# The first modulation rows as TensorE products, and the first input in two halves, in a two-block transformer kernel

## The chip, the cores and the metric

The kernel runs on one core of one Trainium2 chip. Its time is the device time of one execution in microseconds (us). Before the change, three runs took 1449.32, 1450.75 and 1452.83 us; the median is 1450.75 us. The profile shown here is of a separate execution.

## What is computed

Two blocks are applied to 256 tokens of width 1024, in float32. The first mixes an mLSTM with a differential attention and ends in a retrieval of experts; the second has a sparse attention, a convolution and a feed-forward part. The change touches only the start of the first block:

```python
def rmsnorm(x, g):
    xf = x.astype(jnp.float32)
    y = xf * lax.rsqrt(jnp.mean(xf * xf, axis=-1, keepdims=True) + EPS)
    return (y * g.astype(jnp.float32)).astype(x.dtype)
...
    mod = jax.nn.silu(c) @ ada_w[l] + ada_b[l]
    sh1, sc1, g1, sh2, sc2, g2 = jnp.split(mod[:, None, :], 6, axis=-1)

    h = rmsnorm(x, norm1_g[l]) * (1.0 + sc1) + sh1
    p = h @ w_in[l]
    mq, mk, mv, mo, mi, mf, dq, dk, dv = jnp.split(p, split_pts, axis=-1)
```

`ada_w` is 1024 x 6144. `sh1` and `sc1`, the first 2048 of its columns, are needed before the first input `h`; seen as columns of 128 these are 16 "modulation rows", rows 0 to 7 for the shift and 8 to 15 for the scale. The other rows are needed later.

## The kernel before

Everything is held with the features on the 128 partitions: `x` is 8 chunks of 128 x 256. A product in full precision is made of three (`mm3`, L156 to L161): both operands are split into a high and a low part (`hi`, `lo` for the input, `whi`, `wlo` for the weights), and high x high, low x high and high x low are added in PSUM. Weights come by DMA in pairs of units of 128 x 1024 into three buffers named `raw` (`load`, L92). ScalarE (ACT) makes `whi` (L108), VectorE (DVE) makes `wlo` (L116), or both for a few units (L106). `fill` (L97) loads ahead and splits ahead; `w` calls it whenever a unit is taken. Each engine runs its instructions in the order in which they are written, and all loads of this stage are issued from SyncE's queue (SP), in one order.

The start of the first block (`block1_mix`, L419) goes as follows. `silu(c)` is formed on all partitions from a broadcast load of `c` (L430, `silu_vec`). For each modulation row DVE multiplies a 128 x 1024 tile of the transposed `ada_w` with it and sums along the row (`mod_chunk`, L322). The eight scale rows come first, from the `raw` buffers. ACT and TensorE (PE) form the mean square of `x` (`mean_sq`, L280), ACT and DVE its reciprocal root (L257 to L266). Then four times, for two chunks each (L484 to L500): DVE forms two shift rows, ACT forms `hi` (L496), DVE forms `lo` (L499) and scales the next chunks (L481).

`token_major` (L401) multiplies the input with the four units of `w_mv` into two PSUM banks (the tiles named `a`), eight steps k, and behind each step come three products for the gates (`gate`, L512, with `wgate`). Then follow `gates` (L515 to L534), and eight units of `w_mqk`, whose results go through a short convolution (`conv`, tile `cacc`, L550 to L558). The two PSUM banks for units (tiles `m`) come free when `conv` has read them. The rows 16 to 39 are formed later, as chores between units (`mod_chores`, L325).

Of the kernel before, what the change touches and what calls it, by code (L numbers as in the profile page):

```python
# [13 lines left out]
F32 = mybir.dt.float32  # L14
# [5 lines left out]
AF = mybir.ActivationFunctionType  # L20
OP = mybir.AluOpType
# [4 lines left out]
T = 256  # L26
D = 1024
# [28 lines left out]
for _n, _w in (("norm1_g", 8), ("norm2_g", 8), ("final_g", 8), ("norm_mix_g", 8), ("norm_ffn_g", 8),  # L56
               ("ada_b", 48), ("b_ada", 48), ("conv_w", 32), ("conv_b", 8),
               ("mlstm_norm_g", 4), ("diff_norm_g", 1), ("gate_b", 2), ("w_dw", 124), ("b_dw", 4),
               ("conv_ln_g", 4), ("conv_ln_b", 4)):
    SMALL[_n] = (_o, _o + _w)  # L60
    _o += _w
NSMALL = _o
# [2 lines left out]
class Kx:  # L65
# [235 lines left out]
    def pair(self):  # L301
        return [self.normp.tile([128, 8, T], F32R, name=n) for n in ("hi", "lo")]
# [116 lines left out]
    def block1_mix(self):  # L419
        nc, tc, a = self.nc, self.tc, self.a  # L420
        self.mod = [self.const.tile([128, 48], F32, name=f"mod{i}") for i in range(2)]
        mt = self.mod[0]
        with ExitStack() as ctx:
            big = ctx.enter_context(tc.tile_pool(name="b1", bufs=1))
            tmp = ctx.enter_context(tc.tile_pool(name="b1t", bufs=2))
            h = hi, lo = self.pair()
            self.setup()
            self.setup_rows(big)
            craw = tmp.tile([128, D], F32, name="mraw", bufs=2)
            nc.sync.dma_start(craw, self.c_rows(0))  # L430
            self.silu_c[0] = tmp.tile([128, D], F32, name="silu", bufs=1)
            self.silu_vec(0, craw)
            ada = a["ada_w"]
            pair = lambda u: ada[u:u + 2].rearrange("u p f -> p u f")
            held = [big.tile([128, 8, T + 2], F32, name=f"hold{j}") for j in range(4)]
            hold = [t.rearrange("p k t -> p (k t)")[:, :2048].rearrange("p (u f) -> p u f", u=2) for t in held]
            wg = big.tile([128, 8, 36], F32, name="wgate")
            lq = big.tile([128, 4, 64], F32, name="lq")

            def sc_load(j):  # L440
                t = self.wraw.tile([128, 2, 1024], F32, name="raw")
                nc.sync.dma_start(t, pair(8 + 2 * j))
                return t

            sc = [sc_load(j) for j in range(2)]
            nc.sync.dma_start(self.x, a["x"])
            sc.append(sc_load(2))
            nc.sync.dma_start(self.small, a["small"])
            nc.sync.dma_start(wg, a["w_gate"])
            for j in range(4):  # L450
                if j == 3:
                    self.lnexp()
                for i in (1, 0):
                    self.mod_chunk(0, 8 + 2 * j + i, sc[j][:, i], tmp)
                if j == 0:
                    sc.append(sc_load(3))
                elif j == 1:
                    self.load("w_mv", 0)
                    for d in (0, 1):
                        nc.sync.dma_start(hold[d], pair(2 * d))  # L460
                elif j == 2:
                    self.load("w_mv", 2)
                    for d in (2, 3):
                        nc.sync.dma_start(hold[d], pair(2 * d))
                    nc.sync.dma_start(lq, bass.AP(tensor=a["lam"].tensor, offset=a["lam"].offset,
                                                  ap=[[0, 128], [64, 4], [1, 64]]))
            ps = self.side()[:, :T]
            for c in range(8):
                self.mean_sq(ps, self.x[:, c], c, 8, tmp)
            rs = self.rsqrt_start(ps, [128, T], self.normp)  # L470
            rstd = self.rsqrt_end(rs)
            self.mod_bias(0, 8, 16)
            gn = self.make_gain(0, mt[:, 8:16], self.sm("norm1_g"))
            xs = big.tile([128, 8, T], F32, name="xs", tag="yhi")
            wgh = big.tile([128, 8, 36], F32R, name="wgate_h")
            wgl = big.tile([128, 8, 36], F32R, name="wgate_l")
            self.split(wgh, wgl, wg)

            def scaled(j):
                for c in range(2 * j, min(2 * j + 2, 8)):  # L480
                    nc.vector.scalar_tensor_tensor(xs[:, c], self.x[:, c], gn[:, c:c + 1], rstd,  # L481
                                                   op0=OP.mult, op1=OP.mult)

            for j in range(4):  # L484
                if j == 0:
                    self.fill(2, 2)
                elif j == 2:
                    self.fill(4, 4)
                cs = (2 * j, 2 * j + 1)
                if j == 0:  # L490
                    scaled(0)
                for c in reversed(cs):
                    self.mod_chunk(0, c, hold[j][:, c % 2], tmp)
                self.mod_bias(0, cs[0], cs[1] + 1)
                for c in cs:
                    nc.scalar.activation(hi[:, c], xs[:, c], AF.Identity, bias=mt[:, c:c + 1])  # L496
                scaled(j + 1)
                for c in cs:
                    nc.vector.scalar_tensor_tensor(lo[:, c], xs[:, c], mt[:, c:c + 1], hi[:, c].bitcast(F32),  # L499
                                                   op0=OP.add, op1=OP.subtract)  # L500
            heads = lambda t: t.rearrange("p (c t) -> p c t", t=T)

            vm, vd = (hold[0][:, i].rearrange("p (s c) -> p s c", s=2) for i in range(2))
# [2 lines left out]
            ig, fx, ab, B, aa, M, em = (R(n) for n in ("ig", "fx", "ab", "B", "aa", "M", "em"))  # L506
            lf, m = fx, ab
            acol = big.tile([128, 2, 4], F32, name="acol")

            gr = self.side()  # L510

            def gate(k):  # L512
                self.mm3(gr[:36, :T], (wgh[:, k], wgl[:, k]), (hi[:, k], lo[:, k]), k == 0, k == 7)

            def gates():  # L515
                nc.vector.tensor_scalar(ig, gr[:4, :T], gb[:4, 0:1], None, op0=OP.add)
# [16 lines left out]
                yield  # L533
                nc.vector.tensor_copy(acol, p[:, :8].rearrange("p (s h) -> p s h", s=2))  # L534

            self.token_major("w_mv", h, vm, iter([0] * 4), gate)
            self.chores.extend(self.mod_chores([(0, u) for u in range(16, 40)], tmp, 2, nc.sync))
            self.tasks.append(gates())
            self.tick(0)

            qk = [heads(hold[1][:, i]) for i in range(2)]
            cw, cb = self.sm("conv_w"), self.sm("conv_b")
# [86 lines left out]
            for u in range(8):  # L629
                p = self.unit("w_mqk", u, h)  # L630
# [5 lines left out]
            lam = big.tile([128, 2], F32, name="lam")  # L636
# [8 lines left out]
            dg = big.tile([128, 1], F32, name="dg")  # L645
# [72 lines left out]
            for u in range(8):  # L718
                p = self.unit("w_dqk", u, h)
# [3 lines left out]
                else:  # L723
                    for i in range(2):
                        r = slice(64 * i, 64 * i + 64)
# [4 lines left out]
            for u in range(4):  # L730
                p = self.unit("w_mo", u, h)
# [19 lines left out]
            gn = self.make_gain(1, mt[:, 32:40], self.sm("norm2_g"))  # L751
# [752 lines left out]
def _vec(v):  # L1504
    return v.reshape(-1, 128).T


def prepare(**i):
    i = {k: np.asarray(v) for k, v in i.items()}
    w = i["w_in"][0]  # L1510
    o = {}
# [10 lines left out]
    def half(a):  # L1522
# [2 lines left out]
    o["x"] = i["x"][0].T.reshape(8, 128, T).transpose(1, 0, 2)  # L1525
    o["c"], o["c_2"] = i["c"], i["c_2"]
    o["ada_w"] = i["ada_w"][0].T.reshape(48, 128, D)
    o["w_ada"] = i["w_ada_2"][0].T.reshape(48, 128, D)
    g = np.zeros((D, 36), np.float32)
    g[:, :4], g[:, 32:] = mi, mf  # L1530
# [9 lines left out]
    w = i["w_in_2"][0]  # L1540
    q, k, v, qi, ki, wi, ua, ug, ga, gb = np.split(
        w, [512, 1024, 1536, 2048, 2112, 2120, 2632, 3144, 4168], axis=1)
# [5 lines left out]
    f = i["w_ffn_in_2"][0]  # L1548
# [3 lines left out]
    s = np.zeros((128, NSMALL), np.float32)  # L1552

    def put(name, v):
        a, b = SMALL[name]
        s[:v.shape[0], a:b] = v
# [12 lines left out]
    a, b = SMALL["gate_b"]  # L1569
# [2 lines left out]
    put("b_dw", _vec(i["b_dw_2"][0]))  # L1572
    put("conv_ln_g", _vec(i["conv_ln_g_2"][0]))
    put("conv_ln_b", _vec(i["conv_ln_b_2"][0]))
    o["small"] = s
    o["gf"] = i["norm_final_g_2"].reshape(1, D)
    return {k: np.ascontiguousarray(v) for k, v in o.items()}
# [21 lines left out]
```

## Time and profile before

| | before |
|---|---|
| median of three runs | 1450.75 us |
| the profiled execution | 1445.74 us |
| its span, first to last instruction | 1443.7 us |
| PE busy | 1367.2 us, 95% of the span |
| DVE busy | 1098.1 us, 76% |
| ACT busy | 770.9 us, 53% |
| POOL busy | 115.4 us, 8% |
| SP's DMA queue, share of 16 engines | 49.5% |

The span lies 2.0 us below the execution's own time, and that execution lies 5.0 us below the median. Times below are us from the span's start. In a row of the timeline the first number is the start, the second the length, "x2" the number of instructions merged in it, and the bracket the idle time of the engine before it and what ended it. A PE row's length includes the end of the pipeline; from one start to the next is what a product costs in a stream. A float32 product leaves two records on PE, one in the split format leaves one.

### The profile page before, as it was taken

The page shows a single profiled execution, that of the slowest core. Times are in us where ns is not written, and L with a number is a line of the kernel's source. Part 1 is how long each engine was busy: PE and PEld are TensorE (multiplying, and loading weights), DVE is VectorE, ACT ScalarE, POOL GpSimd, SP SyncE. Part 2 cuts the span into 40 slices and gives each one's busy share as a digit, 9 for nine tenths or more (in the row PEclk, how much of TensorE's full clock was granted, in tenths as well). Part 3 has the DMA queues.
Part 4 walks back from the last instruction along what each step waited for, and adds up shares of the span by engine and source line. Part 5 has one row for each costly group of instructions (what it writes and reads, how often), then busy time and mean ns, then how long its engine had stood idle before and what let it go on. Part 6 is the DMA issues. An engine that isn't in the chain of part 4 may idle for free.

```text
span 1443.7 us, 27450 instructions
## 1 busy us (share of the span) xinstructions
PE 1367.2 (95%) x11208; PEld 1321.7 (92%) x11208; DVE 1098.1 (76%) x2105; ACT 770.9 (53%) x1247; POOL 115.4 (8%) x93
## 2 busy tenths in 40 slices
PE   3888999989999999999999999999999899999997
PEld 2767889979999999999999999999999889999997
DVE  7887899996999487777777766666799968765554
ACT  3535665444999545454444454444565484644442
POOL 0020010000000000000000000000167620100000
PEclk8999999999999999999999999999999999999999
DMA  9566554544777888888888867766445335345551
GB/s 376 182 210 216 207 178 147 177 145 146 263 275 280 321 307 291 297 305 315 306 295 283 287 228 240 235 218 219 144 163 175 117 109 208 123 175 190 180 196 64
DMA packets 106062, 317.31 MB, mean 220 GB/s; under 512 B 5584, under 2 KB 34640, under 8 KB 103632
## 3 DMA queue, kind: packets, MB, share of 16 engines
q1 hardware_dynamic: 65696, 250.54, 49.5%
q10 hardware_dynamic: 39408, 61.87, 12.2%
q0 software_dynamic: 832, 3.15, 0.7%
q8 instruction: 88, 1.44, 0.4%
q14 instruction: 38, 0.31, 0.1%
HBM read 297.71 MB, written 17.83 MB: 219 GB/s over the span
## 4 chain that ended last, share of the span: by engine, by line
PE 71%; DVE 21%; ACT 3%; DMA 3%; issue 2%; POOL 0%; POOLq 0%; DVEq 0%; SPq 0%; ACTq 0%
PE m L159 12%; PE m L160 12%; PE m L161 12%; PE a L160 11%; PE a L161 10%; PE a L159 10%; DVE wlo L116 5%; DVE a L1168 3%; DVE junk L322 2%; PE s L983 2%; DMA raw<-in_ada_w 1%; DMA mraw<-in_ada_w 1%; DVE score L1127 1%; DVE cacc L552 1%; ACT whi L108 1%
## 5 line engine op out<-in xcount | busy, mean ns | idle before, releaser
L159 PE MATMUL m<-hi,whi 128*128 128x256 f32 x1816 | 519.3, 286 | 7.1 <-DVE cacc L552 4.0
L161 PE MATMUL m<-hi,wlo 128*128 128x256 f32 x1816 | 509.8, 281 | 2.8 <-POOL wlo L116 1.5
L160 PE MATMUL m<-lo,whi 128*128 128x256 f32 x1816 | 509.6, 281 | 0.0
L116 DVE TENSOR_TENSOR wlo<-raw,whi 128x1024 fp32r<-128x1024 f32 x398 | 479.0, 1222 | 36.3 <-ACT whi L108 25.8
L108 ACT CAST whi<-raw 128x1024 fp32r<-128x1024 f32 x428 | 444.4, 1045 | 50.9 <-DMA raw<-in_peer_v 17.9
L159 PEld LDWEIGHTS m<-hi,whi 128*128 128x128 f32 x1816 | 343.7, 189 | 10.0 <-issue 4.2
L161 PEld LDWEIGHTS m<-hi,wlo 128*128 128x128 f32 x1816 | 343.3, 189 | 3.4 <-DVE wlo L116 1.7
L160 PEld LDWEIGHTS m<-lo,whi 128*128 128x128 f32 x1816 | 343.3, 189 | 0.6
L161 PE MATMUL a<-wh,wlo 128*128 128x256 f32 x1024 | 288.3, 282 | 0.0
L160 PE MATMUL a<-wl,whi 128*128 128x256 f32 x1024 | 288.2, 281 | 0.0
L159 PE MATMUL a<-wh,whi 128*128 128x256 f32 x1024 | 287.9, 281 | 0.0
L161 PEld LDWEIGHTS a<-wh,wlo 128*128 128x128 f32 x1024 | 192.9, 188 | 0.0
L160 PEld LDWEIGHTS a<-wl,whi 128*128 128x128 f32 x1024 | 192.7, 188 | 0.0
L159 PEld LDWEIGHTS a<-wh,whi 128*128 128x128 f32 x1024 | 192.6, 188 | 0.0
L1024 DVE TENSOR_TENSOR wl<-act,wh 128x256 fp32r<-128x256 f32 x128 | 54.5, 425 | 140.5 <-PE a L160 125.2
L790 ACT ACTIVATE act<-m 128x256 f32<-128x256 f32 x126 | 48.4, 384 | 167.2 <-PE m L161 167.2
L1019 ACT CAST wh<-act 128x256 fp32r<-128x256 f32 x128 | 51.9, 406 | 145.4 <-DVE act L1012 121.5
L322 DVE SCALAR_TENSOR_TENSOR junk<-mraw,silu 128x1024 bf16<-128x1024 f32 x80 | 97.5, 1219 | 7.5 <-DMA mraw<-in_ada_w 6.9
L116 POOL TENSOR_TENSOR wlo<-raw,whi 128x1024 fp32r<-128x1024 f32 x33 | 79.2, 2425 | 36.0 <-ACT whi L108 26.5
L986 ACT ACTIVATE stg<-s 128x512 f32<-128x512 f32 x64 | 64.2, 1108 | 3.1 <-PE s L983 1.0
L1012 DVE TENSOR_TENSOR act<-act,gt 128x256 f32<-128x256 f32 x128 | 53.6, 419 | 8.2 <-DMA gt<-gd 8.2
L159 PE MATMUL a<-fh,whi 128*128 128x256 f32 x176 | 50.6, 287 | 3.4 <-ACT fh L250 3.4
(443 smaller groups left out, 1772.8 us busy)
## 6 DMA issues: line engine op xcount, KB each, us to landing
raw<-in_peer_u SPq DMA_DIRECT2D x64, 1024.0 KB, 6.0
raw<-in_peer_v SPq DMA_DIRECT2D x64, 1024.0 KB, 5.1
mraw<-in_w_ada ACTq DMA_DIRECT2D x48, 512.0 KB, 5.5
raw<-in_w_ffn_in SPq DMA_DIRECT2D x22, 1024.0 KB, 5.1
gd<-stg ACTq DMA_DIRECT2D x16, 1024.0 KB, 6.2
gt<-gd ACTq DMA_DIRECT2D x14, 1024.0 KB, 7.5
mraw<-in_ada_w SPq DMA_DIRECT2D x24, 512.0 KB, 4.4
raw<-in_w_ffn_out SPq DMA_DIRECT2D x11, 1024.0 KB, 4.9
```

The costliest lines, as they stand in the source:

```text
L108: self.nc.scalar.copy(t, self.raw[k])
L116: eng.tensor_tensor(t, self.raw.pop(k), h.bitcast(F32), op=OP.subtract)
L159: mm(out, w[0], x[0], start=start, stop=False, **kw)
L160: mm(out, w[0], x[1], start=False, stop=False, **kw)
L161: mm(out, w[1], x[0], start=False, stop=stop, **kw)
L322: self.nc.vector.scalar_tensor_tensor(junk, w, 0.5, self.silu_c[i], op0=OP.mult, op1=OP.mult, accum_out=self.mod[i][:, u:u + 1])
L790: nc.scalar.activation(t, p, AF.Gelu)
L986: nc.scalar.mul(stg[:, :, e0:e0 + 4].rearrange("p i t -> p t i"), p, 1.0 / GSCALE)
L1012: nc.vector.tensor_tensor(tv, tv, gv, op=OP.mult)
L1019: nc.scalar.copy(wts[b], acts[b])
L1024: nc.vector.tensor_tensor(wl, acts.pop(b), wts[b].bitcast(F32), op=OP.subtract)
L1168: nc.vector.scalar_tensor_tensor(zp, z[:, c, k:k + T], w, zp, op0=OP.mult, op1=OP.add)
```

## The change

The 16 rows are formed on PE: the matrix, in its own order, is the moving operand (`ada_n`, cut into eight tiles of 128 x 4 x 512), and `silu(c)`, held as one column of a 32-wide stationary tile (`pad`, tile `junk`) whose other columns are zero, is the stationary one. Four products write to the four quarters of 32 partitions of one PSUM bank, each over half of the sum; ACT copies the bank (L484), and four products with a column of 0.5 turn it into four modulation rows (L487). `row_group(kind, i)` does that for scale (kind 0) or shift (kind 1) of half i. The input is formed in two halves of four chunks (`inputs`), each followed by its half of the products with `w_mv`. `silu(c)` on all partitions, still needed for the later rows, is made between the halves from eight scaled identity blocks and two products with `mean_d` (L530 to L539). `c` is read as a part of `small`.

```diff
+            nc.sync.dma_start(self.small, a["small"])
             nc.sync.dma_start(self.x, a["x"])
+            src = [[rows[:2], rows[2:]]]
+            for kind in range(2):
+                for hf in range(2):
+                    nc.sync.dma_start(src[0][kind][hf], a["ada_n"][(4, 0)[kind] + hf])
+            self.load("w_mv", 0)
             nc.sync.dma_start(wg, a["w_gate"])
-                for i in (1, 0):
-                    self.mod_chunk(0, 8 + 2 * j + i, sc[j][:, i], tmp)
...
+            def row_group(kind, i):
+                g = self.bank(2 + kind)
+                for hf in range(2):
+                    for j in range(4):
+                        mm(g[32 * j:32 * j + 32], pad[:, 4 * hf + j], src[i][kind][hf][:, j], start=hf == 0,
+                           stop=hf == 1, skip_group_check=True)
+                s = tmp.tile([128, 1024], F32, name="mraw", bufs=2)[:, :512]
+                nc.scalar.copy(s, g)
+                p = self.side()
+                for j in range(4):
+                    mm(p[:, j:j + 1], s[:, j * 128:(j + 1) * 128], half, start=True, stop=True, skip_group_check=True)
...
+            def inputs(i):
+                cs = range(4 * i, 4 * i + 4)
                 for c in cs:
-                    nc.scalar.activation(hi[:, c], xs[:, c], AF.Identity, bias=mt[:, c:c + 1])
-                scaled(j + 1)
-                for c in cs:
-                    nc.vector.scalar_tensor_tensor(lo[:, c], xs[:, c], mt[:, c:c + 1], hi[:, c].bitcast(F32),
-                                                   op0=OP.add, op1=OP.subtract)
+                    nc.vector.tensor_scalar(xs[:, c], xs[:, c], gn[:, c:c + 1], mt[:, c:c + 1],
+                                            op0=OP.mult, op1=OP.add)
+                    nc.scalar.copy(hi[:, c], xs[:, c])
+                    if c % 2:
+                        for d in (c - 1, c):
+                            nc.vector.tensor_tensor(lo[:, d], xs[:, d], hi[:, d].bitcast(F32), op=OP.subtract)
...
+            for i in range(2):
+                row_group(0, i)
+                row_group(1, i)
+                if i == 0:
+                    rows_late()
+                    self.split(wgh, wgl, wg)
+                    self.load("w_mv", 2)
+                inputs(i)
+                self.fill(2 * i + 2, 2 * i + 2)
+                for u in (2 * i, 2 * i + 1):
+                    w = self.ready["w_mv", u]
+                    for k in (2 * u, 2 * u + 1):
+                        m = slice(k % 2 * 512, k % 2 * 512 + 512)
+                        for tt in range(2):
+                            s = slice(tt * 128, (tt + 1) * 128)
+                            self.mm3(acc[tt], (hi[:, k, s], lo[:, k, s]), (w[0][:, m], w[1][:, m]), k == 0, k == 7)
+                        gate(k)
+                if i == 0:
+                    dg = tmp.tile([128, 1024], F32, name="mraw", bufs=2)
+                    for k in range(8):
+                        nc.vector.tensor_scalar(dg[:, k * 128:(k + 1) * 128], self.ident, pad[:, k, 0:1], None,
+                                                op0=OP.mult)
+                    self.silu_c[0] = tmp.tile([128, D], F32, name="silu", bufs=1)
+                    for q in range(2):
+                        m = slice(q * 512, q * 512 + 512)
+                        p = self.bank(2 + q)
+                        mm(p, self.mean_d, dg[:, m], start=True, stop=True, skip_group_check=True)
+                        nc.scalar.mul(self.silu_c[0][:, m], p, float(D))
+            for u in range(4):
+                self.w("w_mv", u, False)
...
-            self.token_major("w_mv", h, vm, iter([0] * 4), gate)
-            self.chores.extend(self.mod_chores([(0, u) for u in range(16, 40)], tmp, 2, nc.sync))
+            for tt in range(2):
+                nc.scalar.copy(vm[:, tt], acc[tt])
             self.tasks.append(gates())
             self.tick(0)
+            self.fill(self.pos + 3, self.pos + 2)
+            self.chores.extend(self.mod_chores([(0, u) for u in range(16, 40)], tmp, 2, nc.sync))
```

On SP, the first loads before (`c`, scale rows in `raw`, `x`) stood in this order:

```order
L430 DMA mraw<-in_c 128x1024
L442 DMA raw<-in_ada_w 128x2x1024 x2
L446 DMA x<-in_x 128x2048
L442 DMA raw<-in_ada_w 128x2x1024
L448 DMA small<-in_small 128x319
L449 DMA wgate<-in_w_gate 128x288
L442 DMA raw<-in_ada_w 128x2x1024
L92 DMA raw<-in_w_mv 128x2x1024
```

Now, on SP from its first load on (the four `hold` tiles take the first half's rows):

```order
L441 DMA small<-in_small 128x327
L442 DMA x<-in_x 128x2048
L446 DMA hold_127<-in_ada_n 128x2048
L446 DMA hold_128<-in_ada_n 128x2048
L446 DMA hold_129<-in_ada_n 128x2048
L446 DMA hold_130<-in_ada_n 128x2048
L92 DMA raw<-in_w_mv 128x2x1024
L448 DMA wgate<-in_w_gate 128x288
L454 DMA raw<-in_ada_n 128x2048 x2
```

`x` moved to second place, the scale and shift rows of the first half stand before the first weights, and those of the second half behind.

On PE, the products of the kernel before, from the last mean square on, follow each other with nothing else between them (here the first step of `w_mv` and the start of the second):

```order
L280 MATMUL s<-sq,mean_d 128x256 x8
L159 MATMUL a_283<-whi,hi 128x512
L160 MATMUL a_283<-wlo,hi 128x512
L161 MATMUL a_283<-whi,lo 128x512
L159 MATMUL a_284<-whi,hi 128x512
L160 MATMUL a_284<-wlo,hi 128x512
L161 MATMUL a_284<-whi,lo 128x512
L159 MATMUL s<-hi,wgate_h 36x256
L160 MATMUL s<-lo,wgate_h 36x256
L161 MATMUL s<-hi,wgate_l 36x256
L159 MATMUL a_283<-whi,hi 128x512
```

Now, on PE between the fourth step and the fifth (the bank `a_313` collects scale rows, `a_331` shift rows):

```order
L161 MATMUL m<-hi,wgate_l 36x256
L538 MATMUL a_307<-mraw,mean_d 128x512
L538 MATMUL a_310<-mraw,mean_d 128x512
L481 MATMUL a_313<-raw,junk 32x512 x8
L487 MATMUL s<-half,mraw 128x1 x4
L481 MATMUL a_331<-hold_127,junk 32x512 x4
L481 MATMUL a_331<-hold_128,junk 32x512 x4
L487 MATMUL s<-half,mraw 128x1 x4
L159 MATMUL a_188<-whi,hi 128x512
```

The products that make the second half's modulation rows stand behind the whole first half of the products with `w_mv`, and before the whole second half.

On ACT, around the end of the products with `w_mv`, there stood before (`hold_132` takes the two banks):

```order
L496 ACTIVATE hi<-xs,mod_83 128x256 x4
L108 CAST whi<-raw 128x1024 x2
L496 ACTIVATE hi<-xs,mod_83 128x256 x4
L108 CAST whi<-raw 128x1024 x3
L416 COPY hold_132<-a_283 128x512
L416 COPY hold_132<-a_284 128x512
L517 ACTIVATE fx<-s,small 4x256
```

Now, on ACT over the same place (`hold_127` takes the two banks):

```order
L484 COPY mraw<-a_313 128x512
L484 COPY mraw<-a_331 128x512
L499 CAST hi<-xs 128x256 x4
L108 CAST whi<-raw 128x1024 x2
L575 COPY hold_127<-a_188 128x512
L575 COPY hold_127<-a_189 128x512
L555 ACTIVATE fx<-m,small 4x256
L556 ACTIVATE ab<-fx 4x256
L557 ACTIVATE ab<-ab 4x256
L558 ACTIVATE ab<-ab,one 4x256
L108 CAST whi<-raw 128x1024 x4
```

The splits of the first `w_mqk` units moved from before the copies of the two banks to behind the gates' four ACT instructions, and those of the last two `w_mv` units to behind the last four `hi`.

## Rows read from the trace of the kernel before

**Rows 1.** The chain that ended last, first 130 us: start, length, what.
```profile
8.19 1.24 DVE junk L322 x2
...
41.92 1.15 DVE junk L322 x2
```

**Rows 2.** The timeline of PE, 12 to 50 us.
```profile
29.85 0.80 PE L159 MATMUL a<-whi,hi 128*128 128x512 f32 x1 [10.26 <-ACT hi L496]
...
33.21 0.63 PE L159 MATMUL a<-whi,hi 128*128 128x512 f32 x1
...
35.27 0.39 PE L159 MATMUL a<-whi,hi 128*128 128x512 f32 x1
...
37.01 0.39 PE L159 MATMUL a<-whi,hi 128*128 128x512 f32 x1
...
48.65 0.28 PE L161 MATMUL s<-hi,wgate_l 128*36 128x256 f32 x1
```

**Rows 3.** Busy time by stretch: PE, PEld, DVE, ACT, POOL, granted clock, DMA share, GB/s.
```profile
20.00:30.00 10.00, 0.15 (x1) 0.15 (x1) 9.79 (x22) 3.55 (x7) 0.00 (x0) 0.68 1.03 415
```

**Rows 4.** DMA issues up to 70 us: tile, queue, count, KB each, median us to landing.
```profile
raw<-in_ada_w SPq DMA_DIRECT2D x4, 1024.0 KB, 8.6
...
x<-in_x SPq DMA_DIRECT2D x1, 1024.0 KB, 10.9
...
mraw<-in_c SPq DMA_DIRECT2D x1, 512.0 KB, 4.4
```

**Rows 5.** The timeline of ACT, 12 to 56 us.
```profile
13.16 0.72 ACT L279 ACTIVATE sq<-x 128x256 f32<-128x256 f32 x2 [5.53 <-DMA x<-in_x]
...
19.63 0.47 ACT L257 ACTIVATE rs_t<-s,eps 128x256 f32<-128x256 f32 x1 [0.79 <-PE s L280]
...
21.66 1.99 ACT L108 CAST whi<-raw 128x1024 fp32r<-128x1024 f32 x2 [0.78 <-DMA raw<-in_w_mv]
...
48.21 1.05 ACT L416 COPY hold<-a 128x512 f32<-128x512 f32 x2
50.95 0.47 ACT L517 ACTIVATE fx<-s,small 4x256 f32<-4x256 f32 x1 [1.69 <-DVE ig L516]
...
52.77 1.04 ACT L108 CAST whi<-raw 128x1024 fp32r<-128x1024 f32 x1
```

**Rows 6.** PE, 1175 us: two interleaved column halves (L1302) between other products.
```profile
1175.34 0.28 PE L161 MATMUL m<-hi,wlo 128*128 128x256 f32 x1
1175.55 0.67 PE L1302 MATMUL s<-aTt,v 128*64 128x128 f32 x8
1176.14 0.44 PE L1295 MATMUL s<-ident,S 128*128 128x128 f32 x2
```

**Rows 7.** PE, 1159 us: four float32 products over all 128 columns.
```profile
1159.02 2.00 PE L1187 MATMUL s<-lsq,mean_c 128*128 128x256 f32 x8
```

**Rows 8.** The timeline of DVE, 20 to 57 us.
```profile
22.85 0.16 DVE L349 TENSOR_TENSOR mod<-mod,small 128x8 f32<-128x8 f32 x1
...
23.13 0.45 DVE L251 TENSOR_TENSOR wgate_l<-wgate,wgate_h 128x288 fp32r<-128x288 f32 x1
23.50 2.35 DVE L116 TENSOR_TENSOR wlo<-raw,whi 128x1024 fp32r<-128x1024 f32 x2
...
52.89 0.41 DVE L522 SCALAR_TENSOR_TENSOR fx<-fx,ab 4x256 f32<-4x256 f32 x1 [0.84 <-ACT ab L520]
...
55.87 1.50 DVE L552 SCALAR_TENSOR_TENSOR cacc<-m,small,cacc 128x255 f32<-128x255 f32 x3
```

**Rows 9.** DVE's groups by shape: an operation with two scalars on 128 x 256.
```profile
L1148 DVE TENSOR_SCALAR score<-score 128x256 f32<-128x256 f32 x1 | 0.3, 279 | 0.0
```

**Rows 10.** PE by stretch: length, busy (count), granted clock, DMA share, GB/s.
```profile
20.00:23.60 3.60, 0.00 (x0) 1.00 1.03 420
23.60:30.00 6.40, 0.15 (x1) 0.50 1.03 413
...
33.90:40.00 6.10, 5.02 (x26) 1.00 0.93 343
```

More of the change, by code (lines that the diff above doesn't have):

```diff
@@ L58 @@
                ("mlstm_norm_g", 4), ("diff_norm_g", 1), ("gate_b", 2), ("w_dw", 124), ("b_dw", 4),
-               ("conv_ln_g", 4), ("conv_ln_b", 4)):
+               ("conv_ln_g", 4), ("conv_ln_b", 4), ("c_col", 8)):
     SMALL[_n] = (_o, _o + _w)
@@ L428, in block1_mix @@
             self.setup_rows(big)
[L429 to L434, printed above, removed]
+            flat = lambda t: t.rearrange("p k t -> p (k t)")[:, :2048]
+            quad = lambda t: t.rearrange("p (k f) -> p k f", k=4)
@@ L435, in block1_mix, with row_raw @@
             held = [big.tile([128, 8, T + 2], F32, name=f"hold{j}") for j in range(4)]
-            hold = [t.rearrange("p k t -> p (k t)")[:, :2048].rearrange("p (u f) -> p u f", u=2) for t in held]
+            hold = [flat(t).rearrange("p (u f) -> p u f", u=2) for t in held]
+            rows = [quad(flat(t)) for t in held]
             wg = big.tile([128, 8, 36], F32, name="wgate")
             lq = big.tile([128, 4, 64], F32, name="lq")
-            def sc_load(j):
+            def row_raw():
@@ L441, in sc_load @@
                 t = self.wraw.tile([128, 2, 1024], F32, name="raw")
-                nc.sync.dma_start(t, pair(8 + 2 * j))
-                return t
-            sc = [sc_load(j) for j in range(2)]
+                return quad(t.rearrange("p u f -> p (u f)"))
+            nc.sync.dma_start(self.small, a["small"])
             nc.sync.dma_start(self.x, a["x"])
-            sc.append(sc_load(2))
-            nc.sync.dma_start(self.small, a["small"])
-            nc.sync.dma_start(wg, a["w_gate"])
@@ L450, in block1_mix @@
-            for j in range(4):
-                if j == 3:
-                    self.lnexp()
-                for i in (1, 0):
-                    self.mod_chunk(0, 8 + 2 * j + i, sc[j][:, i], tmp)
[L455 to L466, printed above, removed]
+            src = [[rows[:2], rows[2:]]]
@@ new lines, in block1_mix, with rows_late @@
+            for kind in range(2):
+                for hf in range(2):
+                    nc.sync.dma_start(src[0][kind][hf], a["ada_n"][(4, 0)[kind] + hf])
+            self.load("w_mv", 0)
+            nc.sync.dma_start(wg, a["w_gate"])
+            src.append([[row_raw(), row_raw()], rows[:2]])
+            def rows_late():
+                for kind in range(2):
+                    for hf in range(2):
+                        nc.sync.dma_start(src[1][kind][hf], a["ada_n"][(6, 2)[kind] + hf])
@@ L467, in block1_mix @@
+            pad = tmp.tile([128, 16, 32], F32, name="junk", bufs=1)[:, :8]
+            nc.vector.memset(pad, 0.0)
+            cc = self.sm("c_col")
+            half = big.tile([128, 1], F32, name="half")
+            nc.vector.memset(half, 0.5)
+            ct = tmp.tile([128, 8], F32, name="mx", bufs=4)
+            nc.scalar.activation(ct, cc, AF.Tanh, scale=0.5)
+            nc.vector.scalar_tensor_tensor(pad[:, :, 0], ct, 1.0, cc, op0=OP.add, op1=OP.mult)
+            self.lnexp()
             ps = self.side()[:, :T]
@@ L471, in block1_mix @@
             rstd = self.rsqrt_end(rs)
-            self.mod_bias(0, 8, 16)
-            gn = self.make_gain(0, mt[:, 8:16], self.sm("norm1_g"))
             xs = big.tile([128, 8, T], F32, name="xs", tag="yhi")
@@ L476, in block1_mix @@
             wgl = big.tile([128, 8, 36], F32R, name="wgate_l")
[L477 to L494, printed above, removed]
-                for c in cs:
-                    nc.scalar.activation(hi[:, c], xs[:, c], AF.Identity, bias=mt[:, c:c + 1])
-                scaled(j + 1)
-                for c in cs:
-                    nc.vector.scalar_tensor_tensor(lo[:, c], xs[:, c], mt[:, c:c + 1], hi[:, c].bitcast(F32),
-                                                   op0=OP.add, op1=OP.subtract)
+            mm = nc.tensor.matmul
@@ new lines, in block1_mix @@
+            bias, g1 = self.sm("ada_b"), self.sm("norm1_g")
+            gn = self.gain[:, :8]
+            def row_group(kind, i):
+                g = self.bank(2 + kind)
+                for hf in range(2):
+                    for j in range(4):
[6 more added lines that the diff above has]
+                    mm(p[:, j:j + 1], s[:, j * 128:(j + 1) * 128], half, start=True, stop=True, skip_group_check=True)
+                r = slice((8, 0)[kind] + 4 * i, (8, 0)[kind] + 4 * i + 4)
+                nc.vector.tensor_tensor(mt[:, r], p[:, :4], bias[:, r], op=OP.add)
+                if kind == 0:
+                    nc.vector.scalar_tensor_tensor(gn[:, 4 * i:4 * i + 4], mt[:, r], 1.0, g1[:, 4 * i:4 * i + 4],
+                                                   op0=OP.add, op1=OP.mult)
@@ new lines, in block1_mix, with gate @@
+            gr = self.main()
+            acc = [self.bank(0), self.bank(1)]
+            def gate(k):
+                self.mm3(gr[:36, :T], (wgh[:, k], wgl[:, k]), (hi[:, k], lo[:, k]), k == 0, k == 7)
+            for c in range(8):
+                nc.vector.tensor_tensor(xs[:, c], self.x[:, c], rstd, op=OP.mult)
+            for i in range(2):
[26 more added lines that the diff above has]
+                        nc.scalar.mul(self.silu_c[0][:, m], p, float(D))
@@ L501, in block1_mix @@
+            for u in range(4):
+                self.w("w_mv", u, False)
+            nc.sync.dma_start(lq, bass.AP(tensor=a["lam"].tensor, offset=a["lam"].offset,
+                                          ap=[[0, 128], [64, 4], [1, 64]]))
             heads = lambda t: t.rearrange("p (c t) -> p c t", t=T)
@@ L508, in block1_mix @@
             acol = big.tile([128, 2, 4], F32, name="acol")
-            gr = self.side()
-            def gate(k):
-                self.mm3(gr[:36, :T], (wgh[:, k], wgl[:, k]), (hi[:, k], lo[:, k]), k == 0, k == 7)
             def gates():
@@ L1527, in prepare @@
     o["ada_w"] = i["ada_w"][0].T.reshape(48, 128, D)
+    o["ada_n"] = i["ada_w"][0][:, :2048].reshape(2, 4, 128, 4, 512).transpose(3, 0, 2, 1, 4).reshape(8, 128, 4, 512)
     o["w_ada"] = i["w_ada_2"][0].T.reshape(48, 128, D)
@@ L1574, in prepare @@
     put("conv_ln_b", _vec(i["conv_ln_b_2"][0]))
+    put("c_col", _vec(i["c"][0]))
     o["small"] = s
```

## The prediction

> **What bounds the kernel now.** I read the chain of waits first, then the timelines of the engines on it, in the first 60 us; the part behind them is looked at only for the price of column-packed products. The chain [rows 1] runs from 8.19 to past 41.92 us through the sums on DVE that make the modulation rows; in 20 to 30 us DVE is busy for 9.79 of 10 us and PE for 0.15 [rows 3]. PE starts on `w_mv` at 29.85 us, having waited 10.26 us for the input, and ends the last gate product at 48.65 + 0.28 = 48.93 us [rows 2]; call that point E. From E on, the chain goes through the gates, first on ACT and then on DVE, until DVE starts the first convolution (`cacc`) at 55.87 us [rows 8], 6.94 us behind E. The table in front puts PE at 95% of the whole span, with every stage fed by the one ahead. So a shift of that first `cacc` is a shift of the end unless something later absorbs it, and I work out where E and `cacc` come to lie.
>
> **The change: what goes.** Sixteen sums on DVE (1.15 to 1.24 us each [rows 1]), about 19 us, and the broadcast load of `c`. DVE is then no longer what the input waits for. What is late next is a chain that goes from PE to ACT to PE to DVE to ACT, once for each half.
>
> **Up to the first half's input.** `x` was in at 13.16 us [rows 5], behind 0.52 + 2 x 1.05 MB; with itself 3.67 MB [rows 4]. Now only `small` (0.17 MB) stands ahead: 1.22 MB. At 415 GB/s [rows 3] the 2.45 MB less are 5.9 us: 7.3 us. The next 1.05 MB tiles come 2.5 us apart: the scale rows by 12.4, the shift rows by 17.4, `w_mv` by 19.9, `wgate` by 20.3 us.
> The mean squares are unchanged: 19.63 - 13.16 = 6.47 us from `x` to the end on PE [rows 5], so 13.8 us. A float32 product of 256 columns leaves two records, and eight records take 2.00 us with the pipeline's end [rows 7], about 0.21 us each, or 0.43 for 512 columns. Do four products to four column quarters run side by side? The nearest row has two halves: eight records of 128 columns in 0.67 us [rows 6]. Less the end of the last (0.28), that is four steps of 0.11 us, so they ran in pairs; eight in a row would take 0.75 to the last start alone. I take four side by side: two sets of two records of 0.43, so 1.7 us for a `row_group`, and with switch and end 1.9. The bounds are 3.6 (two by two) and 7.0 (one by one), and nothing better than 1.7, since each set streams 512 columns twice.
> ACT's copy of a 128x512 bank is 1.05 / 2 [rows 5], 0.6 with the handover. The four products with a column of 0.5 leave eight records, each with 128 columns of weights; nearest is the 0.11 us step of rows 6, with the end 1.1 us; bounds 0.5 and 2.
> All of it is serial, because PE runs in program order and the four small products stand ahead of the shift rows: 13.8 + 1.9 + 0.6 + 1.1 = 17.4 for the scale, + 3.6 = 21.0 for the shift. Adding the bias takes 0.16, the split of `wgate`, which stands ahead of the input on DVE, 0.45 [rows 8]: 21.6 us. The input: scaling at 0.28 [rows 9] twice, `hi` at about 0.45 on ACT (taken as `fx` [rows 5]), `lo` as much; the fourth `hi` ends 2.8 us later, 24.4. Only then does ACT split the first weights, 1.99 / 2 us [rows 5], and DVE takes 2.35 / 2 for `wlo` [rows 8]: PE starts at 25.4, and goes on in earnest at 26.6. That is 4.5 us earlier than 29.85.
>
> **The first half, and what stands behind it.** A step k costs 37.01 - 35.27 = 1.74 us at the full clock [rows 2]; four, less the one product done ahead, 6.8: 33.4 us. Two float32 products of 512 columns for `silu`: 1.7, 35.1. Their DVE part (eight 128x128 scalings, under 0.28 each [rows 9]) lies beside the first half. Then the second half's row groups: 2 x (1.9 + 0.6 + 1.1) = 7.2, 42.3. Their data are there (by 30.5 us at the rate above), but PE reaches them only now, and nothing covers them: bias 0.2, input 2.8, `whi` 1.0, `wlo` 1.2, 47.5. The second half 6.8: E at 54.3, against 48.93: **5.4 us later**. The second `w_mv` load on SP waits for the first pair's `wlo` (about 28 us), and all that is queued behind it with it; it lands by 33 us, well ahead of 46.3, so that wait costs nothing. The first two chore loads now stand on SP behind the first `w_dv` load, whose buffer comes free with a `w_mqk` `wlo`, 8 us behind E; the chore that uses them is written behind the fifth convolution, so I count nothing, and a late one would add to the rivals below.
>
> **Behind E.** Before, ACT had split the first `w_mqk` units ahead of E. Now these splits stand behind the two copies and the gates' four ACT instructions. Those wait for the gate products: E + 0.75 for `ig` on DVE, then 1.8 us (52.77 - 50.95 [rows 5]), then 1.0 for the first `whi`: E + 3.6. DVE has four `wlo` in its queue ahead of the gates' second part: 4 x 1.18 = 4.7, E + 8.3. From there to `cacc` it is 55.87 - 52.89 = 3.0 [rows 8]: E + 11.3 in place of 6.94, **4.4 us later**. PE's first two units end by then, so they are hidden.
>
> **The clock.** Before, PE's last mean square ended at 19.6, and the granted clock was still 1.00 up to 23.6 and 0.50 (1.2 GHz) from there; at 33.9, 4 us into the products, it was 1.00 (2.4 GHz) again [rows 10]. Now PE idles from 21.0 to 25.4 and from 42.3 to 46.3. The first gap is longer than those 4.0 us, so I count a fall there: a step then costs 33.21 - 29.85 = 3.36 us [rows 2], and four us at that level, of which 1.2 are waiting, lose 1.5. The second gap is just as long as 4.0; I count nothing, and hold 1.5 as a bound.
>
> **The sum:** 5.4 + 4.4 + 1.5 = 11.3 us later. On the profiled execution that is 1445.74 + 11.3 = 1457.0; that execution lies 5.0 below the median of the runs, so for the median 1450.75 + 11.3 = **1462 us**.
>
> Two rules of the Trainium skill bear on the packed products. The page "TensorE: Matmul & The Clock Gate" (Part 3, Packing small matmuls) states 2.38x for three column tiles. Worked from that figure as an estimate, a group is 1.7 x 3 / 2.38 = 2.2 us and the sum 2 us larger; the pairs of rows 6 show no such loss. Against this change speaks "TensorEngine Tiling (Array Packing)" (Tiling Modes, Key Properties): a change of tiling mode drains TensorE. The trace agrees in kind: from the product at 1175.34 to the first packed one 0.21 us pass [rows 6] in place of 0.12, so eight switches cost under 1 us.
>
> **Rivals.**
> *The products don't run four wide.* Two by two adds 1.7 us to each of four groups: 11.3 + 6.8 = 18.1, 1469 us; one by one adds 5.1 each, 1482. For it: no row here has four quarters, nor 512 float32 columns in each. Against it: the pairs of rows 6.
> *DVE decides after all: faster.* If E is set by DVE's work alone, as rows 1 and 3 show for before, DVE loses 19 us and gains about 2.2 for eight scalings of the input and 1.6 for the identity blocks. E is then some 15 us earlier, less 4.4 behind it: 1440 us. It decides from the point where E falls under 48.9 - 4.4 = 44.5 us. Against it: the second half's `whi` alone can't end before 46.3 in the chain above, and only if PE took the second groups ahead of the first half would that chain shorten; it runs in order.
> *A later stage absorbs it.* The convolutions after 55.87 and the chores wait for loads; where a load isn't later than before, its wait takes up the shift. That gives 1450 to 1457 us. Against it: those loads need buffers that the same chain frees.
>
> **Chances and range.** Forecast 0.64, not four wide 0.15, absorbed 0.11, DVE 0.10. The low end of the forecast's own range has `x` 1 us earlier, small products of 0.5 us (4 x 0.6), and no fall of the clock: +6.4; the high end a second fall: +12.8, and small products of 2 us: +16.4. The range reaches up to two by two and down a little into the absorbed case: 1455 to 1469. About 0.2% (2.9 us) is what a measurement of this kernel can tell from no change. Slower by more: 0.64 + 0.15 + 0.06 of the absorbed case = 0.85; within: 0.05; faster: 0.10.
>
> **What would show it.** PE's first `w_mv` product at 25 to 26 us, an idle stretch of some 4 us on PE between the second half's small products and the fifth step, E at 54 to 56, and ACT's first `w_mqk` split 3 to 4 us behind E, with `cacc` near 67 us. A `row_group` of about 1.9 us shows the packing; 3.6 or 7 the first rival. E under 45 us would make the forecast wrong in its sign, and a later `cacc` with an unchanged end would show absorption.

## The result, and the profile after

| | before | after |
|---|---|---|
| median, 6 runs each on the same chip | 1450.92 us | 1463.16 us |
| lowest to highest | 1449.32 to 1456.25 | 1459.82 to 1466.63 |
| ratio | | 1.0087 (95%: 1.0069 to 1.0105) |
| the profiled execution | 1445.74 | 1462.69 |
| mean granted clock in it | 0.985 | 0.974 |
| first `cacc` on DVE | 55.87 | 69.87 |

The kernel is 12.2 us slower by the medians, where 11.3 were forecast. The profiled execution of after lies 0.5 us below its median, that of before 5.2 below its own. So the two profiles are 17.0 us apart at the end, and the sum is better read at the first `cacc`.

The chain that ended last now begins like this (start, length, what; its pieces of 1.24 us and more, up to 70 us):

```profile
1.26 5.09 DMA x<-in_x
6.84 4.28 PE s L280 x10
13.04 1.90 PE a L481 x16
16.66 1.90 PE a L481 x16
24.47 1.24 DVE wlo L116
35.17 1.72 PE a L538 x4
36.89 1.90 PE a L481 x16
40.55 1.90 PE a L481 x16
48.11 1.24 DVE wlo L116
62.35 4.63 DVE wlo L116 x4
```

None of the sums of [rows 1] is left in it. Instead it goes twice through two row groups (`a` L481) and a `wlo`, and behind the second half through four `wlo` in a row. The timeline of PE at these places (start, length, engine, line; in brackets the idle time before and what ended it):

```profile
12.97 1.92 PE L481 MATMUL a<-hold,junk 128*32 128x512 f32 x16
15.61 1.05 PE L487 MATMUL s<-half,mraw 128*128 128x1 f32 x8 [0.71 <-ACT mraw L484]
...
24.49 0.80 PE L159 MATMUL a<-whi,hi 128*128 128x512 f32 x1 [4.22 <-ACT whi L108]
...
35.01 1.88 PE L538 MATMUL a<-mraw,mean_d 128*128 128x512 f32 x4
36.82 1.92 PE L481 MATMUL a<-raw,junk 128*32 128x512 f32 x16
...
43.11 1.05 PE L487 MATMUL s<-half,mraw 128*128 128x1 f32 x8 [0.70 <-ACT mraw L484]
48.13 0.80 PE L159 MATMUL a<-whi,hi 128*128 128x512 f32 x1 [3.96 <-ACT whi L108]
...
58.42 0.28 PE L159 MATMUL m<-hi,wgate_h 128*36 128x256 f32 x1
```

PE starts 5.4 us earlier than in [rows 2], waits 4 us twice, and its last gate product ends at about 58.94 us (three of them follow at 0.12): E is 10.0 us later. Behind E, on ACT and then on DVE:

```profile
57.93 1.28 ACT L575 COPY hold<-a 128x512 f32<-128x512 f32 x2 [8.90 <-PE a L161]
59.48 0.47 ACT L555 ACTIVATE fx<-m,small 4x256 f32<-4x256 f32 x1 [0.28 <-DVE ig L554]
...
61.29 3.87 ACT L108 CAST whi<-raw 128x1024 fp32r<-128x1024 f32 x4
```

```profile
62.35 4.63 DVE L116 TENSOR_TENSOR wlo<-raw,whi 128x1024 fp32r<-128x1024 f32 x4 [2.30 <-ACT whi L108]
66.90 0.41 DVE L560 SCALAR_TENSOR_TENSOR fx<-fx,ab 4x256 f32<-4x256 f32 x1
...
69.87 1.50 DVE L592 SCALAR_TENSOR_TENSOR cacc<-m,small,cacc 128x255 f32<-128x255 f32 x3
```

From E to `cacc` it is now 10.93 us in place of 6.94 [rows 8]: 4.0 us more. The clock, by stretch (PE busy, granted clock, DMA share, GB/s):

```profile
20.30:24.50 4.20, 0.01 (x1) 0.56 1.02 425
24.50:31.00 6.50, 6.04 (x15) 0.50 0.99 376
31.00:35.00 4.00, 4.00 (x23) 0.99 0.22 70
...
44.20:48.10 3.90, 0.00 (x0) 0.57 0.13 51
48.10:55.20 7.10, 6.61 (x18) 0.52 0.43 148
55.20:59.00 3.80, 3.74 (x21) 1.00 0.00 0
```

In both gaps the clock went from 1.00 (2.4 GHz) to 0.50 (1.2 GHz) soon after PE had stopped: a mean of 0.56 over 4.20 us leaves about 0.5 us at 1.00, and 0.57 over 3.90 us as much. It was back 6.5 and about 7 us after PE's first product behind the gap. Before, it fell once in the stretch up to E, 4.0 us after PE had stopped, and was back 4 us after PE had begun [rows 10]. Behind E it fell once more in both kernels (0.50 from 62 to 68 us now, from 58 to 61 before). The first `cacc` did not wait for that: DVE went into it straight from the gates.

### The profile page after: what moved, and what is told of

The parts are those of the page before. It is cut to its first block, busy times and chain, and to the rows that moved or that the text cites. A ratio compares the mean times of both kernels' runs of the same rounds, so it can differ in the third digit from the quotient of the medians.

```text
span 1460.8 us, 27633 instructions
## 1 busy us (share of the span) xinstructions
PE 1391.4 (95%) x11308; PEld 1336.6 (91%) x11308; DVE 1082.6 (74%) x2091; ACT 772.9 (53%) x1253; POOL 114.7 (8%) x93
## 4 chain that ended last, share of the span: by engine, by line
PE 76%; DVE 18%; ACT 4%; DMA 1%; issue 1%; POOL 0%; POOLq 0%; DVEq 0%; SPq 0%; ACTq 0%
PE m L159 12%; PE m L161 12%; PE m L160 12%; PE a L160 11%; PE a L161 11%; PE a L159 11%; DVE wlo L116 4%; DVE a L1208 3%; PE s L1023 2%; DVE score L1167 1%; DVE cacc L592 1%; ACT whi L108 1%; DMA gt<-gd 1%; PE a L481 1%; DVE junk L322 1%
```

## The experiments

Two theories stood against each other. By the first, the loss is the latency of a serial chain (second row groups that nothing covers, splits put off, `silu` between the halves), with the falls of the clock that its two waits bring. By the rival, it is work: PE is busy for 24.2 us more than the 1367.2 of before, and a kernel that is 95% PE pays for each product. (Not all of the 24.2 us need be work, since at the lower clock the same product keeps PE busy for longer: 0.63 and 0.39 us in [rows 2].) The first line of after's page (busy time, share of the span, instructions):

```profile
PE 1391.4 (95%) x11308; PEld 1336.6 (91%) x11308; DVE 1082.6 (74%) x2091; ACT 772.9 (53%) x1253; POOL 114.7 (8%) x93
```

The ratios are to the kernel before on the same chip, and `cacc` is the start of the first one in its profile, beside 55.87 before and 69.87 after. E is, as above, 0.52 us behind the start of the last step's first gate product: 58.94 after. Diffs are against the changed kernel unless said.

**The `w_mqk` splits ahead of the second half.**

```diff
             for i in range(2):
...
+                if i == 1:
+                    self.load("w_mqk", 0)
+                    self.load("w_mqk", 2)
                 inputs(i)
                 self.fill(2 * i + 2, 2 * i + 2)
+                if i == 1:
+                    self.fill(7, 6)
```

> Edit: the loads and splits of the first w_mqk units are written ahead of the end of the products with w_mv (point E), as in the kernel before; nothing else changes. Serial theory (the loss is latency in the chain up to the first convolution: a second row group nobody covers, deferred splits, clock falls in PE's gaps): the deferred splits cost 4.0 us behind E, so the first cacc comes near 66 us in place of 69.9 and the time falls by 4 us, to about 1459. Work theory (the loss is the 24 us more that PE is busy): no change, 1463.

Measured: 1459.78 us (1457.79 to 1462.05), ratio 1.0066 (1.0051 to 1.0081).

```profile
57.47 0.28 PE L159 MATMUL m<-hi,wgate_h 128*36 128x256 f32 x1
```

```profile
65.52 1.50 DVE L597 SCALAR_TENSOR_TENSOR cacc<-m,small,cacc 128x255 f32<-128x255 f32 x3
```

`cacc` is 4.35 us earlier than after's, but not all of that is the edit's. E, at 57.99, is 0.95 us earlier: the same products of the two halves took less time, since the clock was back sooner in this execution (at 29.5 and 53.4 us, beside 31.0 and 55.0). From E to `cacc` it is 7.53 us in place of 10.93, so the splits ahead gave 3.4 us, where 4.0 were expected and the prediction had 4.4. That term holds for the most part. The time's interval overlaps that of after, here and in the next three runs, so the rows are the sharper measure.

**The gaps filled with products that nobody reads.**

```diff
+                idle = self.side()
+                for _ in range(4):
+                    mm(idle, self.mean_d, self.x[:, :2].rearrange("p c t -> p (c t)"), start=True, stop=True,
+                       skip_group_check=True)
                 inputs(i)
```

> Edit: in each of the two stretches in which PE waits for the input of a half, four more float32 products of 512 columns whose result nobody reads (some 3.5 us each time), so that PE does not idle for 4 us ahead of a half. Serial theory with the clock as a part of it: the granted clock stays at 1.00, each half takes 6.8 us from the first wlo in place of 9.4, and the time falls by 2 x 2.6 = 5 us, to about 1458. Work theory: 7 us more of PE work, 1470. If the clock has no part: 1463.

Measured: 1459.29 us (1456.64 to 1459.54), ratio 1.0056 (1.0040 to 1.0071). Its PE, then DVE:

```profile
20.10 3.68 PE L521 MATMUL s<-x,mean_d 128*128 128x512 f32 x8
...
41.62 3.68 PE L521 MATMUL s<-x,mean_d 128*128 128x512 f32 x8
...
53.49 0.28 PE L159 MATMUL m<-hi,wgate_h 128*36 128x256 f32 x1
```

```profile
64.93 1.50 DVE L596 SCALAR_TENSOR_TENSOR cacc<-m,small,cacc 128x255 f32<-128x255 f32 x3
```

Its clock by stretch (length, busy time and count of PE, PEld, DVE, ACT, POOL, then clock, DMA share, GB/s):

```profile
20.00:25.00 5.00, 4.27 (x12) 1.70 (x11) 3.92 (x11) 3.07 (x7) 0.00 (x0) 1.00 1.02 423
...
45.00:50.00 5.00, 3.81 (x17) 2.55 (x17) 2.55 (x3) 1.62 (x2) 0.00 (x0) 1.00 0.13 18
50.00:55.00 5.00, 4.01 (x22) 2.99 (x20) 0.96 (x2) 1.62 (x3) 0.00 (x0) 1.00 0.47 192
```

PE got 7.4 us of extra work, and the last gate products came 4.93 us earlier (58.42 to 53.49), because the clock stayed at 1.00 through both halves: PE began the first half at the same time (24.45 in place of 24.49), and from E to `cacc` nothing changed (10.92). So about 5 of the 14.0 us between the two profiles are the clock's. The rival's sign is wrong: more work on PE went with an earlier `cacc` and no longer time.

**`silu` behind the second half.** The tile of scaled blocks goes to a buffer that is free (`held[2]`), and the two products with `mean_d` and their reads move from between the halves to behind the gates:

```diff
                 if i == 0:
-                    dg = tmp.tile([128, 1024], F32, name="mraw", bufs=2)
+                    dg = flat(held[2])[:, :1024]
...
-                    for q in range(2):
-                        m = slice(q * 512, q * 512 + 512)
-                        p = self.bank(2 + q)
-                        mm(p, self.mean_d, dg[:, m], start=True, stop=True, skip_group_check=True)
-                        nc.scalar.mul(self.silu_c[0][:, m], p, float(D))
...
             self.fill(self.pos + 3, self.pos + 2)
+            for q in range(2):
+                mq = slice(q * 512, q * 512 + 512)
+                p = self.bank(2 + q)
+                mm(p, self.mean_d, dg[:, mq], start=True, stop=True, skip_group_check=True)
+                nc.scalar.mul(self.silu_c[0][:, mq], p, float(D))
```

> Edit: the two products that spread silu(c), and ACT's reading of them, are moved from between the two halves to behind point E, where PE waits anyway (the scaled identity blocks stay where they are, in another tile). Serial theory: 1.8 us of PE come off the chain, so E, the first cacc and the end come 1.8 us earlier, about 1461. Work theory: the same PE work, 1463.

Measured: 1461.48 us (1458.36 to 1466.04), ratio 1.0075 (1.0055 to 1.0095).

```profile
55.18 0.28 PE L159 MATMUL m<-hi,wgate_h 128*36 128x256 f32 x1
...
55.53 1.88 PE L577 MATMUL a<-hold,mean_d 128*128 128x512 f32 x4
...
66.62 1.50 DVE L592 SCALAR_TENSOR_TENSOR cacc<-m,small,cacc 128x255 f32<-128x255 f32 x3
```

`cacc` moved by 3.25 us in the one profile, and E (55.70) by as much. The products explain 1.8 of it; the first half began 0.45 us earlier (24.04), and the second half's products took 0.9 us less, again with the clock back sooner. The median moved by 1.7 us, but its runs lie from 1458 to 1466, so it does not tell that from nothing.

**The second half's row groups inside the first half.** With `silu` late as above, `row_group` is cut in two: `row_mm` (eight products) and `row_end` (copy, small products, bias). For the second half they stand between the first steps k:

```diff
                         gate(k)
+                        if k == 0:
+                            late = row_mm(0, 1)
+                        elif k == 1:
+                            row_end(0, 1, late)
+                            late = row_mm(1, 1)
+                        elif k == 2:
+                            row_end(1, 1, late)
```

> Edit: as silu late, and the second half's row groups are written between the steps of the first half of the products with w_mv, so that ACT and DVE make the second half's input while PE works. Serial theory: the second half's first weights are split near 44 us, E comes near 51.5 us in place of 58.9, the first cacc near 62.5, and the time falls by about 7 us against the changed kernel, to 1456. Work theory: the same work, 1463.

Measured: 1458.97 us (1452.66 to 1462.93, 8 runs), ratio 1.0058 (1.0038 to 1.0078). The second half's first product on PE, the first `cacc` on DVE, and two stretches (as above):

```profile
42.96 0.50 PE L159 MATMUL a<-whi,hi 128*128 128x512 f32 x1 [2.12 <-ACT whi L108]
```

```profile
63.72 1.50 DVE L602 SCALAR_TENSOR_TENSOR cacc<-m,small,cacc 128x255 f32<-128x255 f32 x3
```

```profile
41.00:43.00 2.00, 0.04 (x1) 0.04 (x1) 1.35 (x5) 1.76 (x4) 0.00 (x0) 1.00 0.00 0
43.00:47.00 4.00, 3.24 (x10) 2.21 (x11) 2.30 (x2) 0.86 (x1) 0.00 (x0) 0.69 0.17 19
```

The second half starts 5.17 us earlier (48.13 to 42.96), of which 1.8 are the products for `silu`, and `cacc` 6.15. The median gained 4.2 us where 7 were expected. The profile shows one reason: the clock still fell, behind a wait of 2.1 us, and `cacc` came 1.2 us later than expected. Whether that is the whole shortfall is open, since its runs spread over 10 us.

**Both: rows inside and splits ahead.** The two edits above together.

> Edit: rows inside and splits ahead together. Serial theory: the two gains lie at different places of one chain and add up: the first cacc at 63.7 - 4.0 = 59.7 us, the time 4 us under rows inside, about 1455. Work theory: no change against rows inside, 1459.

Measured: 1456.64 us (1452.84 to 1462.19, 12 runs), ratio 1.0037 (1.0021 to 1.0053). The second half on PE, from its first product to the last step's first gate product, then DVE:

```profile
43.01 0.69 PE L159 MATMUL a<-whi,hi 128*128 128x512 f32 x1 [2.12 <-ACT whi L108]
...
53.38 0.28 PE L159 MATMUL m<-hi,wgate_h 128*36 128x256 f32 x1
```

```profile
58.41 1.23 DVE L116 TENSOR_TENSOR wlo<-raw,whi 128x1024 fp32r<-128x1024 f32 x1 [2.88 <-ACT whi L108]
...
62.53 1.50 DVE L607 SCALAR_TENSOR_TENSOR cacc<-m,small,cacc 128x255 f32<-128x255 f32 x3
```

`cacc` came at 62.53, where 59.7 was expected. The miss of 2.8 us lies at two places. The second half begins when it does with the rows inside alone (43.01 and 42.96), but E comes 1.1 us later (53.90 and 52.79): the clock fell in the second wait again, and was lower for longer (0.50 from 44 to 48 us). From E to `cacc` it is 8.63 us, so the splits ahead gave 2.3 us in place of 4.0. Here DVE waits 2.88 us for a `whi` that stands on ACT behind the two reads for `silu` (1.09 us); in the first experiment, where those reads were done between the halves, that wait was 1.78 us. So the two gains did not simply add up.

**The weights first.** On top of the last kernel, ACT makes both `whi` of each half, and DVE the first `wlo`, before the input is formed. The kernel before did so with its first two units [rows 5]:

```diff
                     self.load("w_mqk", 2)
+                self.fill(2 * i + 2, 2 * i + 1)
                 inputs(i)
```

> Edit: as rows and splits, and the first weights of each half are split ahead of the input of that half in place of behind it. Serial theory: 2 us of ACT and 1.2 of DVE come off the chain ahead of the first half, and the 2.1 us in which PE waited for the second half's weights go: the first cacc near 55.5 us, about where it is in the kernel before, and the time about 1451. Work theory: 1459.

Measured: 1447.24 us (1445.18 to 1455.12, 12 runs), ratio 0.9981 (0.9967 to 0.9995). PE at the start of both halves, then the first `cacc`:

```profile
22.72 0.80 PE L159 MATMUL a<-whi,hi 128*128 128x512 f32 x1 [2.53 <-ACT hi L502]
...
38.22 0.50 PE L159 MATMUL a<-whi,hi 128*128 128x512 f32 x1 [0.31 <-ACT hi L502]
```

```profile
54.12 1.50 DVE L608 SCALAR_TENSOR_TENSOR cacc<-m,small,cacc 128x255 f32<-128x255 f32 x3
```

A stretch of the second half, and the first line of the page (busy time, share, instructions):

```profile
35.00:40.00 5.00, 4.69 (x29) 3.63 (x27) 3.60 (x9) 2.34 (x6) 0.00 (x0) 1.00 0.41 161
```

```profile
PE 1381.9 (96%) x11306; PEld 1329.7 (92%) x11308; DVE 1082.5 (75%) x2091; ACT 773.6 (54%) x1253; POOL 114.9 (8%) x93
```

This one line gave the most: 9.4 us in the median and 8.4 at `cacc`, all of the latter ahead of E (45.49 in place of 53.90). The first half starts 2.9 us earlier, the second 4.8; the second wait is down to 0.31 us, and the clock is at 1.00 from 30 to 50 us. The expectation counted too little by 1.4 us at `cacc` and by some 4 us in the time. PE has the same products to do as after and is busy for 9.5 us less (1381.9 in place of 1391.4). So at most 14.7 of the 24.2 us are work; the rest fits the lower clock of after's profile (mean 0.974, here 0.983).

**The first gap filled too.** The last kernel with three products that nobody reads ahead of the first half's input (as in the second experiment).

> Edit: as weights first, with three float32 products of 512 columns, whose result nobody reads, in the stretch in which PE waits for the first input. Serial theory with the clock: the first half runs at the full clock, 2 us less: the first cacc near 53.5 us, the time about 1449, under the kernel before. Work theory: 2.6 us more work, 1461. If the clock has no part here: 1451.

Measured: 1446.73 us (1444.93 to 1451.58, 12 runs), ratio 0.9975 (0.9963 to 0.9986).

```profile
36.70 0.50 PE L159 MATMUL a<-whi,hi 128*128 128x512 f32 x1 [0.30 <-ACT hi L502]
...
43.45 0.28 PE L159 MATMUL m<-hi,wgate_h 128*36 128x256 f32 x1
```

```profile
52.61 1.50 DVE L612 SCALAR_TENSOR_TENSOR cacc<-m,small,cacc 128x255 f32<-128x255 f32 x3
```

The first line of its page (busy time, share, instructions):

```profile
PE 1386.0 (96%) x11312; PEld 1332.7 (92%) x11314; DVE 1082.7 (75%) x2091; ACT 772.7 (54%) x1253; POOL 113.8 (8%) x93
```

It beats both kernels, with PE busy for 18.8 us more than before (1386.0 - 1367.2). Against the kernel without the filling `cacc` is 1.5 us earlier, and the times don't differ by what can be measured. Behind its last gate product it still loses time: DVE waits 2.89 us for a `whi` that stands on ACT behind the two reads for `silu`. Moving those was not tried.

Put side by side, in the order of `cacc` (each in us against after's 69.87 and 1463.16; the runs are from more than one chip, on which the kernel before had medians of 1450.25 to 1451.37, so the medians compare to about 1 us):

| | `cacc` | median |
|---|---|---|
| `silu` late | -3.3 | -1.7 |
| splits ahead | -4.4 | -3.4 |
| gaps filled | -4.9 | -3.9 |
| rows inside | -6.2 | -4.2 |
| rows and splits | -7.3 | -6.5 |
| before | -14.0 | -12.2 |
| weights first | -15.8 | -15.9 |
| first gap filled too | -17.3 | -16.4 |

The end follows the first `cacc` in this order, at half to all of its size. That bears out the prediction's first step, and leaves little for the rival: the last two kernels have all the added work and are faster than the one before, so work does not order these kernels.

## Why the prediction was right, and where it was off

*The sign and its cause: right.* The sums on DVE went, and a chain that goes twice through PE, ACT and DVE in turn came in their place.

*Up to the first half: right within 1 us.* `x` came at 6.37 us in place of 7.3. A row group took 1.92 (1.9), the copy 0.59 (0.6), the small products 1.05 (1.1); PE started at 24.49 (25.4). The four quarters ran side by side, so the first rival fell: 16 records in 1.92 us, where a 512-column record by itself is 0.43 (the four of L538 above take 1.88 us), and 16 would be 6.9. The estimate of 2.2 us by the Trainium skill's "TensorE: Matmul & The Clock Gate" (Part 3, Packing small matmuls), drawn from its 2.38x for three column tiles, is above what these rows show.

*The second half's uncovered chain, 5.4 us: right.* Without the clock E would lie at 54.3 less the 0.9 of `x`, 53.4. The run in which the clock stayed up put it at 53.49 + 0.52 = 54.0, counting from its first gate product as above.

*The clock, 1.5 us: the step that was mis-sized.* It was counted for the first gap only, which was held to be longer than the 4.0 us between stop and fall in the profile of before, and for 4 us at half clock. It fell in both gaps, about 0.5 us after PE had stopped, so the length of the gap did not tell the two apart; and it was back only after 6.5 and 7 us. From the first `wlo` on, the first half took 35.01 - 25.75 = 9.3 us and the second as long, each 2.5 above the 6.8 at the full clock: 5 in place of 1.5. The second fall stood in the text as a bound. So E came at 58.94, past the 54 to 56 that were named. What a fall costs differs between executions. From the first `wlo` product to the last step's first gate product a half took 6.5 us with the gaps filled; against that the two falls together cost 4.9 us in after's profile, 3.5 in that of the splits ahead (1.5 and 2.0) and 3.8 in that of `silu` late. So the price of one fall was low but near, and the count of falls was wrong.

*Behind E, 4.4 us: right.* The two profiles gave 4.0, of which the first experiment took back 3.4.

*The sum.* At `cacc` 14.0 us in place of 11.3: 3.5 more for the clock, 0.9 less for `x`, 0.4 less behind E, and some 0.5 more from steps that were each longer by under 0.2 than counted. By the medians it is 12.2. That this lies within 1 us of the forecast is in part luck, since the sum was 2.7 short where it was worked out. Which of the missing 1.8 us are given back later and which are the spread of single executions the profiles can't tell, since that of before was a low one.

*The other rivals fell.* DVE did not decide, since E came later and not 15 us earlier. The shift was not absorbed as a whole: in every run the end moved the way of `cacc`. Whether a later stage takes up a part of it stays open.

*What the prediction priced but did not single out* is that the change put the split of each half's first weights behind its input. In the sum that was 1.0 + 1.2 us in each half. Its undoing, tried only on top of the other edits, was worth 8.4 us at `cacc`: in its profile most of the second wait is gone, and with it the fall of the clock there.

## What to carry to other kernels

Shortening the busiest engine's share of a start-up stage helps only if what replaces it is not more serial: write down, for each half or tile, which engine hands to which, and do all that needs no input (weight splits, next tile's side products) ahead of that chain. Price a wait on TensorE with the slower products that follow it as well as with its own length, and do so for every wait, not only for the first. A stage's first dependent instruction downstream (here `cacc`) tells sooner and more sharply than the total whether an edit of one us or two has worked. Split the way to it at a point in between (here E): in a single profile it also carries what the clock did in that execution, 0.95 us in the first experiment.

## What the runs showed of the hardware

Four float32 products of 512 columns to the four quarters of the columns ran at the same time: 16 records in 1.92 us, where one by itself takes 0.43. Products with a single moving column and 128 columns of float32 weights cost about 0.13 us a record (1.05 us for eight, with the end of the pipeline).

In the profile of after the granted clock took longer to come back than in the one of before: 6.5 and 7 us after PE had begun again, beside 4. The time from PE's stop to the fall differed too: about 0.5 us beside 4.0. With the rows inside, alone and with the splits ahead, it fell though PE had waited only 2.1 us just before, while in the kernel before it stayed at 1.00 behind a wait of 2.0 us (to 40.93 us); why, no run here settles.
